# Routed experts on one core: the second product's tiles alternate with the next expert's first product, and small experts use one PSUM bank per unit

## The chip, the cores and the metric

The kernel runs on one core of a Trainium2 chip. The metric is the device time of one execution in microseconds, as the median of several executions. A profiled execution gives the trace that is read below; its times are microseconds from the start of its span.

## The reference, cut to what matters

The kernel computes one layer of a hybrid encoder for 1024 tokens of width 1024: a mixing half (recurrent heads and stick-breaking attention), which the change does not touch, and then 32 routed experts, of which each token uses four. For the experts the reference reads:

```python
def expert_block(args):
    tok, gate, e = args
    xb = xt[tok]
    hid = xb @ w1[e] + b1[e]                                  # 1024 -> 2048
    glu = jnp.minimum(hid[:, :D_FF_EXPERT], SWIGLU_LIMIT)
    lin = jnp.clip(hid[:, D_FF_EXPERT:], -SWIGLU_LIMIT, SWIGLU_LIMIT)
    act = glu * jax.nn.sigmoid(SWIGLU_ALPHA * glu) * (lin + 1.0)
    return (act @ w2[e] + b2[e]) * gate[:, None]              # 1024 -> 1024
out = jax.ops.segment_sum(y.reshape(n_rows, d), row_tok, num_segments=n_tok)
```

All weights are float32, 12.6 MB for one expert, and every expert's weights are read once. The precision is kept by splitting: a weight is a high part (`whi`, 32-bit) plus a low part (`wlo`, bf16), and the rows of an expert likewise.

## The kernel before, in words

Experts are sorted by their number of tokens, and each rank has a fixed capacity `c` of slots: 128 for the 13 smallest, 136 to 184 for the other 19. The kernel takes them in the order `ORDER`, largest and smallest in turn, so that for the first 26 experts one with more than 128 slots alternates with one of 128; the last six all have more than 128. Within this order `j` counts the experts.

An expert's weights come as six tiles of 2 MB: four of the first product, `(j, 1, q)` with q = 0 to 3 (q = 0 and 2 are the gate side, 1 and 3 the linear side of the two halves of the hidden width), and two of the second product, `(j, 2, 0)` and `(j, 2, 1)`. Each tile is two units, h = 0 and 1, and the list of units is the program order. The text writes A0 to A3 for the first product's tiles of an expert, S0 and S1 for the second's. The list `order` in `expert_units` (L1362 to L1367) is before: A1 A2 A3 of expert j, A0 of expert j + 1, then S0 S1 of expert j.

What happens for a unit, and where:

- `w_load` (L1371) issues a tile's load on SyncE's queue. There are WRAW = 4 raw buffers, so the load of a tile waits until the tile four places before it in the list is free. A first-product tile is free when VectorE has made the low parts of both its units (`next_lo`, L1538); a second-product tile is free only when TensorE has finished its second unit (`experts`, L1585 to L1588), since its raw form is itself multiplied. Loads are issued in the list's order.
- `w_hi` (L1411, ScalarE) makes the high part three units ahead of its use, `w_lo` (L1429, VectorE) the low part two units ahead. The first unit of S0 needs neither; it multiplies the raw weights.
- `first` (L1431) multiplies a first-product unit: for each of two blocks b of 128 hidden columns eight matmuls with the high weights over 2c columns (L1439) and eight with the low weights over c columns (L1443). Its accumulator `hid` is two PSUM banks, one for each block, and there are two such buffers, so that a unit waits until the unit two before it has been read out. The readout is two ScalarE activations (L1449) and one VectorE addition (L1450).
- `gated` (L1452) makes the activations after q = 1 and q = 3; `second` (L1480) multiplies by the second weights (L1500), and for an expert of more than 128 slots the remaining slots by the raw weights (L1506), and then scales and scatters the rows to the output (L1513 to L1522, GpSimd's indirect DMA with addition).
- `rows` (L1279) finds, beside A0 of expert j, which tokens expert j + 1 gets: a count by matmuls (L1308), some small VectorE steps, and an indirect DMA that gathers the rows (`xg`, L1327, GpSimd). `x_transpose` (L1331) turns those rows by TensorE transposes (L1344), the first group right behind the second unit of A1 in the program.

All of this is written in one program order; a planner then lays out each engine's instruction list, with its own estimates of durations, and every engine runs its list strictly in that order. PSUM is full: `hid` 4 banks, `ey` 2, `er` 1, `xt` 1, and the last is shared by the counts and the transposes.

Of the kernel before, what the change touches and what calls it, by code (L numbers as in the profile page):

```python
# [9 lines left out]
FT = mybir.dt.float32  # L10
# [17 lines left out]
NE = 32  # L28
# [86 lines left out]
class Trunk:  # L115
# [1241 lines left out]
    def expert_units(self, xs):  # L1357

        order = [(0, 1, 0)]  # L1362
        for j in range(NE):
            order += [(j, 1, q) for q in (1, 2, 3)]
            if j + 1 < NE:
                order.append((j + 1, 1, 0))
            order += [(j, 2, 0), (j, 2, 1)]  # L1367
        tiles = [Box(x=xs[j], w=w, q=q, i=i, raw=None) for i, (j, w, q) in enumerate(order)]
        return tiles, [Box(t=t, h=h) for t in tiles for h in range(2)]

# [60 lines left out]
    def first(self, u, pool, psum):  # L1431

        nc, x, t = self.nc, u.t.x, u.t
        half, g = divmod(t.q, 2)
        c, f = x.c, 8 * g + 4 * half + 2 * u.h
        ps = psum.tile([128, 2, 512], FT, name="hid", bufs=2)
        for b in range(2):
            for k in range(ND):
                nc.tensor.matmul(ps[:, b, :2 * c], u.hi[:, k, b * 128:(b + 1) * 128],  # L1439
                                 x.X2[:, k].rearrange("p a c -> p (a c)"), start=k == 0, stop=False)  # L1440
        for b in range(2):
            for k in range(ND):
                nc.tensor.matmul(ps[:, b, :c], u.lo[:, k, b * 128:(b + 1) * 128], x.xb[:, k, :],  # L1443
                                 start=False, stop=k == ND - 1)
        if u.h == 0:
            x.t[g] = pool.tile([128, 4, c], FT, name="ht", bufs=3, tag="ht")
        dst = x.t[g][:, 2 * u.h:2 * u.h + 2]
        for b in range(2):
            nc.scalar.activation(dst[:, b], ps[:, b, c:2 * c], AF.Identity, bias=x.bias[:, f + b:f + b + 1])  # L1449
        nc.vector.tensor_tensor(dst, dst, ps[:, :, :c], op=OP.add)  # L1450
# [29 lines left out]
    def second(self, u, pool, psum):  # L1480


        nc, x, t = self.nc, u.t.x, u.t
        first, last = t.q == u.h == 0, t.q == u.h == 1
        n1 = self.rest(x.c)
        nj = 128 // n1 if n1 else 0
# [365 lines left out]
```

## Time and profile before

| | |
|---|---|
| time, median of 3 executions | 2505.66 us (2494.64 to 2509.85) |
| time of the profiled execution | 2492.26 us |
| its span | 2490.4 us |
| TensorE matmul busy | 2346.1 us, 94% of the span |
| VectorE busy | 1977.9 us, 79% |
| ScalarE busy | 1573.8 us, 63% |
| mean granted TensorE clock | 0.969 |
| the units of the experts | from about 1088 us to about 2482 us |

The median tells the time; the profiled execution tells where it goes. Its own time is 13.4 us below the median, so a sum that is made on its rows is carried over to the median as a difference.

### The profile page before, as it was taken

The page shows a single profiled execution, that of the slowest core. Times are in us where ns is not written, and L with a number is a line of the kernel's source. Part 1 is how long each engine was busy: PE and PEld are TensorE (multiplying, and loading weights), DVE is VectorE, ACT ScalarE, POOL GpSimd, SP SyncE. Part 2 cuts the span into 40 slices and gives each one's busy share as a digit, 9 for nine tenths or more (in the row PEclk, how much of TensorE's full clock was granted, in tenths as well). Part 3 has the DMA queues.
Part 4 walks back from the last instruction along what each step waited for, and adds up shares of the span by engine and source line. Part 5 has one row for each costly group of instructions (what it writes and reads, how often), then busy time and mean ns, then how long its engine had stood idle before and what let it go on. Part 6 is the DMA issues. An engine that isn't in the chain of part 4 may idle for free. (4 is left out here: it accounts for less than half of the span.)

```text
span 2490.4 us, 49823 instructions
## 1 busy us (share of the span) xinstructions
PE 2346.1 (94%) x19973; PEld 1770.9 (71%) x19973; DVE 1977.9 (79%) x3639; ACT 1573.8 (63%) x2467; POOL 239.6 (10%) x182
## 2 busy tenths in 40 slices
PE   6889999999999899979999999999999999999997
PEld 2456676667676665667787787878788878887875
DVE  5567668669687767678888898898899989998885
ACT  3525556557676645346676676777677767776673
POOL 0000000000000000001111112111111112121111
PEclk8989999999999799979999999999999999999999
DMA  8774343333232312567798898889899989998994
GB/s 294 255 243 125 106 115 112 107 97 92 73 105 73 107 45 89 185 212 279 280 350 280 290 363 314 319 310 346 310 325 333 362 310 329 345 350 292 317 339 129
DMA packets 321007, 579.57 MB, mean 233 GB/s; under 512 B 46527, under 2 KB 110021, under 8 KB 320741
## 3 DMA queue, kind: packets, MB, share of 16 engines
q1 hardware_dynamic: 304768, 532.21, 60.1%
q0 software_dynamic: 14304, 43.53, 7.0%
q8 instruction: 159, 2.61, 0.4%
q10 hardware_dynamic: 1700, 0.61, 0.1%
q14 instruction: 76, 0.61, 0.1%
HBM read 517.69 MB, written 58.61 MB: 231 GB/s over the span
## 5 line engine op out<-in xcount | busy, mean ns | idle before, releaser
L1411 ACT ACTIVATE whi<-wraw 128x2048 fp32r<-128x2048 f32 (+1 forms) x361 | 675.4, 1876 | 376.1 <-PE ey L1500 158.3
L1429 DVE TENSOR_TENSOR wlo<-wraw,whi 128x2048 bf16<-128x2048 f32 (+1 forms) x361 | 805.4, 2234 | 112.0 <-PE ey L1500 67.9
L1439 PE MATMUL hid<-X,whi 128*128 128x256 f32 (+7 forms) x4096 | 628.9, 305 | 38.0 <-DVE ht L1450 36.0
L1439 PEld LDWEIGHTS hid<-X,whi 128*128 128x128 f32 x4096 | 561.4, 191 | 74.3 <-issue 63.9
L1443 PE MATMUL hid<-xb,wlo 128*128 128x128 bf16 (+7 forms) x4096 | 299.1, 226 | 0.0
L1443 PEld LDWEIGHTS <-wlo 128*128 128x128 bf16 x4096 | 251.9, 98 | 18.2
L338 PE MATMUL zps<-hhi,zwlo 128*128 128x512 f32 x416 | 246.5, 592 | 0.0
L336 PE MATMUL zps<-hhi,zwhi 128*128 128x512 f32 x416 | 188.5, 453 | 20.8 <-DVE zlast L380 8.0
L1449 ACT ACTIVATE ht<-hid,b1r 128x128 f32<-128x128 f32 (+7 forms) x496 | 158.6, 373 | 17.0 <-PE hid L1443 17.0
L337 PE MATMUL zps<-hlo,zwhb 128*128 128x512 bf16 x416 | 167.9, 404 | 1.4 <-DVE hlo L247 1.4
L1500 PE MATMUL ey<-whi,ah 128*128 128x512 f32 x384 | 143.9, 456 | 0.0
L1327 POOL DMA_INDIRECT xg<-h2d,si x49 | 79.1, 1614 | 573.8 <-PE ey L1500 321.6
L1500 PE MATMUL ey<-wraw,act 128*128 128x512 f32 x256 | 125.6, 611 | 1.3 <-SPq L1826 1.3
L1515 POOL DMA_INDIRECT out_dram<-ey,si x32 | 104.4, 3262 | 206.2 <-DVE ey L1513 177.4
L1450 DVE TENSOR_TENSOR ht<-ht,hid 128x256 f32<-128x256 f32 (+7 forms) x256 | 114.3, 447 | 10.4 <-ACT ht L1449 8.9
L1500 PE MATMUL ey<-whi,al 128*128 128x512 f32 x384 | 120.6, 395 | 0.0
L336 PEld LDWEIGHTS zps<-hhi,zwhi 128*128 128x128 f32 x416 | 82.4, 198 | 53.2 <-issue 21.4
L337 PEld LDWEIGHTS <-zwhb 128*128 128x128 bf16 x416 | 42.1, 101 | 93.2 <-issue 87.9
L1500 PE MATMUL ey<-wlo,ab 128*128 128x512 bf16 x384 | 99.6, 382 | 0.0
L1500 PEld LDWEIGHTS ey<-whi,ah 128*128 128x128 f32 x384 | 70.9, 189 | 39.4 <-issue 23.8
L514 DVE TENSOR_TENSOR_SCAN se<-se 128x128 f32<-128x128 f32 (+3 forms) x96 | 92.9, 971 | 0.7
L244 ACT ACTIVATE zwhi<-zwraw 128x1024 fp32r<-128x1024 f32 x50 | 52.8, 1055 | 61.1 <-PE zps L336 46.4
(475 smaller groups left out, 4124.8 us busy)
## 6 DMA issues: line engine op xcount, KB each, us to landing
wraw<-in_exp_w_dram SPq DMA_DIRECT2D x189, 2048.0 KB, 12.1
zwraw<-in_w_in_dram SPq DMA_DIRECT2D x50, 512.0 KB, 4.1
aw<-in_ada_w_dram SPq DMA_DIRECT2D x32, 512.0 KB, 5.3
zr<-zo SPq DMA_DIRECT2D x28, 256.0 KB, 3.6
zs<-zo SPq DMA_DIRECT2D x24, 256.0 KB, 2.1
nx<-in_x_dram SPq DMA_DIRECT2D x8, 512.0 KB, 7.3
awh<-in_ada_w_dram SPq DMA_DIRECT2D x8, 512.0 KB, 4.9
mx<-in_x_dram SPq DMA_DIRECT2D x16, 256.0 KB, 3.1
```

Of the source, the lines that this page charges most:

```text
L336: nc.tensor.matmul(ps, hi[:, k], self.hhi[:, k, s], start=k == 0, stop=False)
L337: nc.tensor.matmul(ps, hb[:, k], self.hlo[:, k, s], start=False, stop=False)
L338: nc.tensor.matmul(ps, lo[:, k], self.hhi[:, k, s], start=False, stop=k == ND - 1)
L514: nc.vector.tensor_tensor_scan(er, er, er, initial=carry, op0=OP.add, op1=OP.bypass)
L1411: nc.scalar.activation(dst[:, k], src[:, k], AF.Copy)
L1429: nc.vector.tensor_tensor(dst[:, k], src[:, k], hi[:, k], op=OP.subtract)
L1439: nc.tensor.matmul(ps[:, b, :2 * c], u.hi[:, k, b * 128:(b + 1) * 128], x.X2[:, k].rearrange("p a c -> p (a c)"), start=k == 0, stop=False)
L1443: nc.tensor.matmul(ps[:, b, :c], u.lo[:, k, b * 128:(b + 1) * 128], x.xb[:, k, :], start=False, stop=k == ND - 1)
L1449: nc.scalar.activation(dst[:, b], ps[:, b, c:2 * c], AF.Identity, bias=x.bias[:, f + b:f + b + 1])
L1450: nc.vector.tensor_tensor(dst, dst, ps[:, :, :c], op=OP.add)
L1500: nc.tensor.matmul(x.ps[n], a[:, j, :128], w[:, j, n * 512:(n + 1) * 512], start=first and m == 0, stop=last and m == len(products) - 1)
L1515: nc.gpsimd.indirect_dma_start(out=rows, out_offset=bass.IndirectOffsetOnAxis(ap=x.idx[:, 0:1], axis=0), in_=y, in_offset=None, compute_op ...
```

## The change

The list of tiles becomes: the four first-product tiles of expert 0, and then for every expert j: A0 of expert j + 1, S0 of expert j, A1 of expert j + 1, S1 of expert j, A2 and A3 of expert j + 1. So the two second-product tiles of an expert no longer follow each other. For experts of at most 128 slots the accumulator is allocated once for a tile (two units) and each unit uses one of its two banks, half a bank for each block of 128 columns; the eight high and eight low matmuls of the first block are then finished before those of the second block begin. Larger experts keep their accumulator and their order of matmuls. The numbers of buffers, the loads, the readouts and everything else stay as they are.

```diff
-        order = [(0, 1, 0)]
+        order = [(0, 1, q) for q in range(4)]
         for j in range(NE):
-            order += [(j, 1, q) for q in (1, 2, 3)]
-            if j + 1 < NE:
-                order.append((j + 1, 1, 0))
-            order += [(j, 2, 0), (j, 2, 1)]
+            n = [(j + 1, 1, q) for q in range(4)] if j + 1 < NE else []
+            order += [*n[:1], (j, 2, 0), *n[1:2], (j, 2, 1), *n[2:]]
...
-        ps = psum.tile([128, 2, 512], FT, name="hid", bufs=2)
-        for b in range(2):
+
+        small = c <= 128
+        if u.h == 0 or not small:
+            t.ps = psum.tile([128, 2, 512], FT, name="hid", bufs=2)
+        ps = t.ps[:, u.h].rearrange("p (b n) -> p b n", b=2) if small else t.ps
+
+        def high(b):
             for k in range(ND):
                 nc.tensor.matmul(ps[:, b, :2 * c], u.hi[:, k, b * 128:(b + 1) * 128],
                                  x.X2[:, k].rearrange("p a c -> p (a c)"), start=k == 0, stop=False)
-        for b in range(2):
+
+        def low(b):
             for k in range(ND):
                 nc.tensor.matmul(ps[:, b, :c], u.lo[:, k, b * 128:(b + 1) * 128], x.xb[:, k, :],
                                  start=False, stop=k == ND - 1)
+
+        for part, b in ((high, 0), (low, 0), (high, 1), (low, 1)) if small else ((high, 0), (high, 1), (low, 0), (low, 1)):
+            part(b)
```

## Rows read from the trace of the kernel before

**Rows 1.** Engines' busy time over 1150 to 2450 us, sum of four stretches:

```profile
sum 1300.00, PE 1262.12 PEld 1039.02 DVE 1146.99 ACT 920.87 POOL 221.18; mean PE 315.53 PEld 259.75 DVE 286.75 ACT 230.22 POOL 55.30
```

**Rows 2.** TensorE's groups, 1150 to 2450 us; busy, mean ns, idle before, releaser:

```profile
L1439 PE MATMUL hid<-X,whi 128*128 128x256 f32 x1632 | 234.7, 295 | 29.1 <-DVE ht L1450 28.8
...
L1439 PE MATMUL hid<-X,whi 128*128 128x288 f32 x512 | 79.4, 306 | 1.6 <-DVE ht L1450 1.5
L1439 PE MATMUL hid<-X,whi 128*128 128x272 f32 x464 | 67.0, 295 | 5.8 <-DVE ht L1450 5.7
```

**Rows 3.** TensorE's list in time around one stall; start, duration, idle before it:

```profile
1691.31 1.20 PE L1439 MATMUL hid<-X,whi 128*128 128x256 f32 x8
1692.35 1.07 PE L1443 MATMUL hid<-xb,wlo 128*128 128x128 bf16 x16
1696.25 2.26 PE L1439 MATMUL hid<-X,whi 128*128 128x256 f32 x9 [2.83 <-DVE ht L1450]
```

**Rows 4.** ScalarE's list in time around the same stall:

```profile
1692.92 1.91 ACT L1411 ACTIVATE whi<-wraw 128x2048 fp32r<-128x2048 f32 x1 [3.57 <-DMA wraw<-in_exp_w_dram]
...
1695.04 0.61 ACT L1449 ACTIVATE ht<-hid,b1r 128x128 f32<-128x128 f32 x2
```

**Rows 5.** SyncE's issues of weight loads, in time:

```profile
1673.21 0.37 SPq L1382 DMA_DIRECT2D wraw<-in_exp_w_dram  x1
1680.73 0.37 SPq L1382 DMA_DIRECT2D wraw<-in_exp_w_dram  x1
```

**Rows 6.** TensorE's list in time, end of S0 and of S1, and two units:

```profile
1661.28 0.63 PE L1308 MATMUL xt<-aux,oh 128*128 128x5 bf16 x16
...
1671.09 1.94 PE L1506 MATMUL er<-wraw,act 128*32 128x256 f32 x32
...
1680.49 2.17 PE L1439 MATMUL hid<-X,whi 128*128 128x256 f32 x16
...
1683.38 2.15 PE L1439 MATMUL hid<-X,whi 128*128 128x256 f32 x16
1685.38 1.07 PE L1443 MATMUL hid<-xb,wlo 128*128 128x128 bf16 x16
1686.28 0.61 PE L1344 MATMUL xt<-ident,xg 128*128 128x128 f32 x4
```

**Rows 7.** Stretches: length, engines busy (instructions), granted clock, DMA share, GB/s:

```profile
1650.00:1666.00 16.00, 16.00 (x166) 14.95 (x166) 15.32 (x26) 13.82 (x22) 0.00 (x0) 1.00 1.01 387
1666.00:1674.00 8.00, 8.00 (x55) 4.38 (x54) 7.52 (x17) 3.24 (x4) 2.96 (x2) 1.00 0.20 56
```

**Rows 8.** One stretch of 50 us with a lower granted clock, same columns:

```profile
1650.00:1700.00 50.00, 47.03 (x430) 38.92 (x430) 42.88 (x64) 33.70 (x49) 8.31 (x4) 0.97 0.86 308
```

**Rows 9.** TensorE's list in time from a count of rows to its transposes:

```profile
1625.23 0.34 PE L1308 MATMUL xt<-aux,oh 128*128 128x5 bf16 x8
...
1630.66 0.82 PE L1500 MATMUL ey<-whi,ah 128*128 128x512 f32 x2
...
1636.15 2.70 PE L1439 MATMUL hid<-X,whi 128*128 128x320 f32 x16
...
1643.32 0.60 PE L1344 MATMUL xt<-ident,xg 128*128 128x128 f32 x4
```

**Rows 10.** GpSimd's list in time: gathers (L1327) and the scatter behind one:

```profile
1630.08 1.00 POOL L1327 DMA_INDIRECT xg<-h2d,si  x1 [21.77 <-issue]
1638.01 3.37 POOL L1515 DMA_INDIRECT out_dram<-ey,si  x1 [6.93 <-DMA xg<-h2d,si]
1670.74 1.00 POOL L1327 DMA_INDIRECT xg<-h2d,si  x1 [29.35 <-PE ey L1500]
```

**Rows 11.** A readout that waited for its matmuls: TensorE, ScalarE and VectorE in time:

```profile
1703.45 1.07 PE L1443 MATMUL hid<-xb,wlo 128*128 128x128 bf16 x16
...
1704.55 0.63 ACT L1449 ACTIVATE ht<-hid,b1r 128x128 f32<-128x128 f32 x2 [1.84 <-PE hid L1443]
...
1707.10 0.41 DVE L1450 TENSOR_TENSOR ht<-ht,hid 128x256 f32<-128x256 f32 x1
```

## The prediction

> **What bounds the kernel now.** I read the stretches first, since the change touches only the experts. Over 1300 us of them TensorE is busy for 1262.12, VectorE for 1146.99 (88%) and ScalarE for 920.87 [rows 1]: the stage goes at TensorE's pace, and what can be won without taking work away is its 37.88 us of idle time. The groups of TensorE by shape say where that idle time lies: 28.8 us before the high matmuls of experts with 128 slots, 5.7 and 1.5 before those with 136 and 144, none worth naming elsewhere, and all of it ended by the readout's addition on VectorE, that is, by a full accumulator [rows 2]. TensorE's list in time has the 28.8 us as 13 stalls of 1.5 to 2.8 us, one in each small expert, of which one stands in [rows 3].
>
> What stands behind that releaser is read from the lists in time around one of them. TensorE ends a unit, then stands for 2.83 us [rows 3]. ScalarE had meanwhile waited 3.57 us for a weight tile, and the readout that TensorE needed was queued behind that wait on ScalarE; it began at 1695.04 [rows 4]. The tile's load had been issued at 1680.73 [rows 5], a quarter of a microsecond after TensorE finished S1 [rows 6]: it needed S1's raw buffer. The load before it was issued at 1673.21, right after the end of S0 at 1673.03 [rows 5, 6]. So both second-product tiles hold their buffers until TensorE has gone through them, one behind the other, and the loads starve: the DMA engines move 387 GB/s up to 1666 us and 56 in the eight microseconds after it [rows 7], and then the tiles come late. It is a bunching of loads, not a lack of bandwidth.
>
> **The change part by part.**
>
> *The order.* By the buffers' rule the load of tile i waits for tile i - 4. Before, A3 and then the next A0 wait for S0 and S1, which end 7.5 us apart (1673.03 and 1680.49 [rows 6]), and A0 is wanted two tiles after S1's end. After, S0 lets in A3, and the next A0 follows it at once; S1 lets in the next S0, which lies four tiles ahead. From the end of S0 to A3's first unit lie A1, S1 and A2, six units. At 2.9 us for a small unit (1680.49 to 1683.38 [rows 6]) that is over 17 us, minus 1.9 for the high part [rows 4], while the late load took 12.2 (1680.73 to 1692.92 [rows 4, 5]). ScalarE wants the high part some three units earlier, about 9 us after the issue, but it only holds back readouts that TensorE needs two units later. So no load should come later than the readouts can bear, and I take the small experts' 28.8 us as gone. What replaces them as the last is TensorE's own work: VectorE at 88% and ScalarE at 71% [rows 1] have room. The 7.2 us of the last large experts [rows 2] stand in a run with no small expert in it; their bounds are 0 and 7.2, and I take half, 3.6.
>
> *The clock.* After the stall of 2.83 us nine matmuls took 2.26 us where eight took 1.20 before it [rows 3]: 0.9 us lost in them, the engine at 1.2 instead of 2.4 GHz for a while. Four stretches of 50 us, each with one of the longer stalls, show 0.97 [rows 8], which is 1.5 us at most. Between 0.9 and 1.5 I take 1.3, four times: 5.2 us, gone with the stalls.
>
> *The bank per unit.* It gives a small expert's unit three or more units of distance to the readout in its way instead of two. That is a second cover for the same 28.8 us and is not counted twice. Its cost: TensorE changes from high to low and back once more in each unit. Eight high matmuls behind such a change take 1.04 us (1691.31 to 1692.35 [rows 3]), sixteen take 2.00 (1683.38 to 1685.38 [rows 6]), so the last eight take 0.96 and the change costs 0.08. There are 13 experts with 8 units, 104 changes: 8.3 us, on the engine that sets the pace, with nothing to hide it. The low part is wanted one microsecond earlier in the unit; VectorE makes it two units ahead, which covers that.
>
> *What else is moved.* The transposes of expert j + 1 stand behind A1, and between the count of rows and A1 there is now S0 alone, no longer S0 and S1. For a small next expert the transposes began 18.1 us after the count (1625.23 to 1643.32), of which S1 takes 5.5 (1630.66 to 1636.15 [rows 9]): 12.6 remain. The rows had landed by 1638.01, when the scatter queued behind them on GpSimd went on [rows 10]: 12.8 after the count. For a large next expert it is 25.0 (1661.28 to 1686.28) minus 7.5 for S1 [rows 6], 17.5 us, and the gather is issued 9.5 us after the count and lands up to 7.9 later (as 1630.08 to 1638.01 [rows 10]): 17.4. So the distance shrinks to about zero. If the count also moves behind A0's second unit, which it now precedes, 2.9 us more go, so the wait lies between 0 and 2.8 us for each of 30 gathers. Behind a waiting transpose stands all of TensorE's list. I take 0, since the gather will be issued just before S0 lets the loads in, on DMA engines that are then little used; the upper end is 84 us. The scatters on GpSimd and the loads on SyncE keep their order.
>
> **Sum.** -28.8 - 3.6 - 5.2 + 8.3 = -29.3 us. The profiled execution's 2492.26 us would become 2463; from the median of 2505.66 it is 2476 us, 1.2% less. The three times of before lie 15 us apart, so within 1% (25 us) counts as no change.
>
> **The rivals.**
>
> *The transposes wait for their rows.* Slower. Place: TensorE in front of the first transposes (L1344), ended by the gather's DMA. At the full 2.8 us it gives 2476 + 84 = 2560; it decides from 1.0 us for each gather, where the 29.3 are used up, and ends above 1% from 1.8 us. For it: the two margins of about zero. Against it: the planner may lay later matmuls in front of the transposes, and the gather is issued before the loads. 0.20, of which 0.05 stays within 1%.
>
> *The two halves of the accumulator count as one buffer*, so that the change doesn't do what it says. A readout of block 0 lies in another bank than block 1, and yet it started at 1704.55 when all sixteen low matmuls of the unit, begun at 1703.45, were through [rows 11]. If matmuls into the second bank likewise wait for the first bank's readout, each of 52 second units waits at least 0.63 + 0.41 us [rows 11]; in A0 and A1 the planner has units of S to put between, so 26 of them count: 27 us, 2503. With nothing between it is 54 and 2530. 0.12, of which 0.02 is above 1%.
>
> The Trainium skill speaks against this rival (PSUM — Partial Sum Buffer, PSUM bank collisions raise a hardware error): it asks for a guard by bank and quadrant, and has an engine reading one bank while TensorE writes another run clean. By that rule nothing on the chip asks for the wait and 2476 stands; the row above shows a wait for the whole of the two-bank tile, and no row shows the reverse, a write beside a readout of the same tile.
>
> *The stalls come back from VectorE.* At 88% and in strict order it may miss a readout by itself once the loads are in time. Half of the stalls stay: 2476 + 16 = 2492. 0.13.
>
> *More is won.* All 7.2 us of the large experts go, and the alternation spreads VectorE's low parts, four tiles of A in a row becoming three, so that the other small waits go too and half of the changes from high to low are hidden in them: 2460 to 2470. 0.10.
>
> **How the numbers follow.** The forecast has 0.45, of which 0.05 stays within 1%, since it lies only 4 us beyond. Faster by over 1%: 0.40 + 0.10 = 0.50. Slower: 0.15 + 0.02 = 0.17. The rest is 0.33. The range reaches down to 2455, the best case with all bounds and some 5 us of spread, and up to 2535, which takes in the second rival whole and the first up to 2 us for each gather; what it leaves out is the heavy end of the first and the scatter of the median, together 0.2.
>
> **What would show it.** Right: the idle time before L1439 by VectorE's readout is near zero, ScalarE's waits for `wraw` are short, issues of loads come in pairs with no stretch at 56 GB/s before a late tile, and the group of 128x256 matmuls costs some 8 us more between its starts. Wrong: idle time before L1344 with a gather as its releaser, or before the second unit of a small tile with its own first readout as releaser.

## The result, and the profile after

The changed kernel takes 2514.6 us (median of 12 runs) where the kernel before takes 2499.1 (12 runs on the same chip): a ratio of 1.0066, with an interval of 1.0048 to 1.0083. That is 0.7% slower, under the 1% that counted as a change, but outside the uncertainty, and on the other side of the forecast of 2476. One of the 12 runs took 5650 us and is left out of the ratio; nothing here explains it. The profiled execution has a span of 2512.50 us against 2490.43; the profile of before is a quick one among its runs (2492.26 us, 6.8 under the median).

TensorE's groups by shape, 1150 to 2450 us, after (they answer to [rows 2]):

```profile
L1442 PE MATMUL hid<-X,whi 128*128 128x256 f32 x1605 | 246.4, 296 | 6.5 <-DVE ht L1457 6.2
L1447 PE MATMUL hid<-xb,wlo 128*128 128x128 bf16 x1608 | 125.3, 221 | 7.8 <-DVE wlo L1427 7.8
...
L1442 PE MATMUL hid<-X,whi 128*128 128x320 f32 x512 | 85.8, 321 | 5.5 <-DVE ht L1457 5.1
L1442 PE MATMUL hid<-X,whi 128*128 128x288 f32 x512 | 80.8, 312 | 10.3 <-DVE ht L1457 10.3
L1442 PE MATMUL hid<-X,whi 128*128 128x304 f32 x384 | 63.5, 320 | 6.3 <-DVE ht L1457 6.2
...
L1344 PE MATMUL xt<-ident,xg 128*128 128x128 f32 x278 | 43.5, 275 | 5.2 <-DMA xg<-h2d,si 5.1
```

and the sum of four stretches over the same time (as [rows 1]):

```profile
sum 1300.00, PE 1248.22 PEld 1025.95 DVE 1127.82 ACT 907.80 POOL 186.17; mean PE 312.05 PEld 256.49 DVE 281.96 ACT 226.95 POOL 46.54
```

The small experts' idle time before the high matmuls fell from 28.8 us to 6.2, nearly as forecast, and what is left is of another kind (below). But the large experts, which had 7.2 us before ([rows 2]: 5.7 and 1.5), now have 24.5 (5.1, 10.3, 6.2 of it in the three rows), the small ones wait 7.8 us for low parts, which they never did, and 5.1 us are waits for gathered rows. TensorE is busy for 1248.22 us of the 1300, less than the 1262.12 of [rows 1].

**The second half waits for the first.** This is TensorE's list in time for a small expert's tiles A2 and A3, after:

```profile
1601.09 1.22 PE L1442 MATMUL hid<-X,whi 128*128 128x256 f32 x8
...
1604.44 1.19 PE L1442 MATMUL hid<-X,whi 128*128 128x256 f32 x8
1606.21 0.62 PE L1447 MATMUL hid<-xb,wlo 128*128 128x128 bf16 x8 [0.58 <-DVE wlo L1427]
...
1609.07 1.22 PE L1442 MATMUL hid<-X,whi 128*128 128x256 f32 x8 [0.78 <-DVE ht L1457]
...
1612.74 1.51 PE L1442 MATMUL hid<-X,whi 128*128 128x256 f32 x8
...
1615.99 2.60 PE L1442 MATMUL hid<-X,whi 128*128 128x320 f32 x16
...
1622.56 2.74 PE L1442 MATMUL hid<-X,whi 128*128 128x320 f32 x9 [2.84 <-DVE ht L1457]
```

and VectorE's, in the same time, a low part and the addition queued behind it:

```profile
1606.40 2.28 DVE L1427 TENSOR_TENSOR wlo<-wraw,whi 128x2048 bf16<-128x2048 f32 x1
1608.61 0.41 DVE L1457 TENSOR_TENSOR ht<-ht,hid 128x256 f32<-128x256 f32 x1
```

By the program's own numbers of tiles and weights, 1601.09 is A2's first unit, 1604.44 is A3's first, 1609.07 is A2's second, and 1612.74 A3's second. The addition that reads A2's first unit ends at 1608.61 + 0.41 = 1609.02, and A2's second unit starts 0.05 us later, though it writes the other bank. The list of instructions has the wait written out: the second unit's first matmul waits for VectorE (here A2 and A3 of another small expert).

```
12425 L1442 MATMUL hid_22457<-X2_21852,whi_22385 128x256 [waits DVE_49]
12463 L1442 MATMUL hid_22553<-X2_21852,whi_22453 128x256 [waits DVE_49]
```

Laid against the trace, instruction by instruction, all 52 second units of small experts' tiles begin after the first unit's addition, none less than 53 ns after it and 31 of them within 53 to 56 ns (the 35 in the expectation of E5 below is a miscount). In the list all 52 wait for VectorE. The planner knows this wait and puts A3's first unit between A2's units, which is the swapped order seen above; that unit is then wanted before its low part is there (the 0.58).

**The loads still come late.** SyncE's issues of weight loads, after:

```profile
1601.22 0.37 SPq L1386 DMA_DIRECT2D wraw<-in_exp_w_dram  x1
1601.85 0.37 SPq L1380 DMA_DIRECT2D wraw<-in_exp_w_dram  x1
```

ScalarE's list, after:

```profile
1614.37 0.39 ACT L1353 ACTIVATE xb<-xt 128x256 bf16<-128x256 f32 x1
1618.92 1.91 ACT L1409 ACTIVATE whi<-wraw 128x2048 fp32r<-128x2048 f32 x1 [4.16 <-DMA wraw<-in_exp_w_dram]
...
1621.35 0.60 ACT L1456 ACTIVATE ht<-hid,b1r 128x128 f32<-128x128 f32 x2
```

S1 of the expert before lets in the next S0 at 1601.22 (L1386 loads a second-product tile, L1380 one of the first product), and 0.63 us later follows A1 of the large expert. By the program's list the tile that ScalarE waits for here is this A1: it wants it from 1614.76 (1618.92 - 4.16), 12.9 us after its issue, and has it after 17.1. S0, issued first, was used at 1611.79 without a wait for its load. The loads are moved one behind the other: in the trace's DMA packets S0's (4 KB each) start up to 1609 and A1's (2 KB) only from 1608, and up to 1612 a scatter's packets go beside them. Behind ScalarE's wait is queued a readout (1621.35), and TensorE, now in the large expert's A0, stands for 2.84 us (1622.56). It is the stall of [rows 3, 4] in another place. Before, the late tile was the first of its pair: A0, issued at 1680.73 [rows 5], with S0's load right behind it:

```profile
1681.37 4.99 SPq L1388 DMA_DIRECT2D wraw<-in_exp_w_dram  x2
```

Over the whole stage ScalarE waits 74.6 us for weights, 46.2 of it for A1; before it was 65.2, 36.6 of it for A0. The median load takes 14.0 us to land instead of 12.1 (of the 50 whose landing the trace tells).

What a stall of that length does to the clock, in stretches of 10 us, after (length, engines busy, granted clock, DMA share, GB/s):

```profile
1610.00:1620.00 10.00, 9.71 (x95) 8.76 (x93) 8.55 (x9) 4.69 (x9) 2.24 (x1) 1.00 1.04 362
1620.00:1630.00 10.00, 7.44 (x43) 6.79 (x44) 5.47 (x8) 7.43 (x14) 0.00 (x0) 0.66 0.82 302
```

A mean of 0.66 is some 6.8 of the 10 us at 1.2 GHz, the rest at 2.4.

**The ledger.** For each profiled execution, from TensorE's list in time: the stage from the first matmul of the first product to the end of the last `ey` matmul; idle time (pauses over 0.1 us) by what ended it, readouts apart for small and large experts; work, which is the stage less the idle time; and the time in the stage at 1.2 GHz. In us; small items are left out of the middle columns.

| kernel | stage | idle | readouts small / large | low part | rows | X2 | work | at 1.2 GHz |
|---|---|---|---|---|---|---|---|---|
| before | 1386.1 | 39.7 | 28.8 / 7.2 | 0 | 0 | 1.3 | 1346.4 | 17.4 |
| after | 1414.2 | 52.5 | 6.3 / 24.5 | 7.8 | 5.2 | 6.9 | 1361.7 | 41.5 |
| e1 order alone | 1380.4 | 39.3 | 2.8 / 24.4 | 0 | 10.0 | 0.6 | 1341.1 | 14.1 |
| e2 bank alone | 1449.8 | 75.2 | 61.4 / 9.5 | 0 | 0 | 1.7 | 1374.6 | 85.7 |
| e3 more alternation | 1402.7 | 36.6 | 25.6 / 5.8 | 0 | 0 | 2.4 | 1366.1 | 31.1 |
| e4 spaced | 1468.9 | 83.5 | 0.3 / 2.9 | 0 | 37.0 | 11.2 | 1385.4 | 83.0 |
| e5 own banks, new order | 1393.2 | 41.6 | 0 / 2.5 | 0 | 35.2 | 2.8 | 1351.6 | 30.8 |
| e6 own banks, old order | 1378.5 | 31.9 | 0 / 9.8 | 0 | 0 | 21.3 | 1346.5 | 10.6 |
| e7 order, late transposes | 1371.2 | 29.9 | 7.9 / 4.6 | 0 | 0 | 16.5 | 1341.3 | 13.9 |
| e8 order, half loads | 1338.5 | 5.0 | 0.6 / 0.6 | 0 | 1.9 | 0.6 | 1333.5 | 3.8 |
| e9 own banks, late transposes | 1361.8 | 14.6 | 0 / 3.3 | 0 | 0 | 10.8 | 1347.3 | 10.4 |
| e10 own banks, early rows | 1361.0 | 17.2 | 2.5 / 7.9 | 0 | 4.8 | 1.3 | 1343.8 | 13.8 |
| e11 order, early rows | 1370.8 | 30.1 | 0 / 25.9 | 1.4 | 0 | 2.0 | 1340.7 | 24.1 |
| e12 after, half loads | 1347.6 | 7.3 | 0.3 / 0.6 | 0 | 0.6 | 0.6 | 1340.4 | 3.8 |

Against the order alone the changed kernel has 13.2 us more idle time and 20.6 more work. Of the time at 1.2 GHz TensorE is busy for 39.2 and 14.0 us; at half the clock it does half, so that an estimated 12.6 us of the work is the lower clock. 8.0 are left for the alternation of high and low matmuls. The same sum gives 2.7 for E2 and 3.0 for E6 against before, 3.1 for E5 against E1, 7.1 for E9 against E7 and 7.5 for E10 against E11.

### The profile page after: what moved, and what is told of

Same layout as the page of the kernel before. It is cut to its first block, busy times and chain, and to the rows that moved or that the text cites. A ratio compares the mean times of both kernels' runs of the same rounds, so it can differ in the third digit from the quotient of the medians.

```text
span 2512.5 us, 49732 instructions
## 1 busy us (share of the span) xinstructions
PE 2353.7 (94%) x19973; PEld 1776.9 (71%) x19973; DVE 1978.2 (79%) x3639; ACT 1577.4 (63%) x2467; POOL 206.8 (8%) x182
## 5 line engine op out<-in xcount | busy, mean ns | idle before, releaser
L1442 PE MATMUL hid<-X,whi 128*128 128x256 f32 (+7 forms) x4096 | 654.6, 309 | 39.1 <-DVE ht L1457 30.4
L1442 PEld LDWEIGHTS hid<-X,whi 128*128 128x128 f32 x4096 | 573.0, 193 | 85.9 <-issue 52.2
L1447 PE MATMUL hid<-xb,wlo 128*128 128x128 bf16 (+7 forms) x4096 | 320.7, 228 | 7.8 <-DVE wlo L1427 7.8
L1522 POOL DMA_INDIRECT out_dram<-ey,si x32 | 84.8, 2650 | 467.0 <-DVE ey L1520 465.7
L1327 POOL DMA_INDIRECT xg<-h2d,si x49 | 72.9, 1487 | 394.7 <-issue 156.2
L526 PEld LDWEIGHTS sbo<-sbv,sat 128*128 128x128 f32 x576 | 76.5, 195 | 18.4 <-ACT sat L524 9.5
```

The lines of the kernel that those rows point to most:

```text
L1522: nc.gpsimd.indirect_dma_start(out=rows, out_offset=bass.IndirectOffsetOnAxis(ap=x.idx[:, 0:1], axis=0), in_=y, in_offset=None, compute_op ...
```

## The experiments

All ratios are to the kernel before, timed on the same chip in the same session; the interval stands behind.

**E1 and E2, the two parts alone.** E1 is the kernel before with the first piece of the diff above alone (the order). E2 has the second piece alone (the accumulators and their order of matmuls); its list of tiles is that of before:

```diff
 E2, against the changed kernel
...
-            order += [*n[:1], (j, 2, 0), *n[1:2], (j, 2, 1), *n[2:]]
+            order += [(j, 1, q) for q in (1, 2, 3)]
...
+            order += [(j, 2, 0), (j, 2, 1)]
```

> The new order alone, accumulators as before. Theory P (parts: the loss is some 8 us of switches between high and low, some 9 us of lowered clock and some 12 us of new idle time, because loads issued in pairs share the DMA engines and a second-product tile still comes late): without the switches 8 us of the loss go, but the small experts lose the spare bank as well, so 0.2% to 0.6% slower than before, idle time before the high matmuls at 30 us or more. Rival B (the order does what was forecast and the bank with its split blocks does the harm): 1.0% to 1.4% faster than before, idle time under 10 us.

> The bank per unit alone, in the order of before. Theory P: the small experts' units get room, so most of the 28.8 us before their high matmuls go and 5 us of clock with them, against 8.3 us of switches: 0.7% to 1.0% faster than before. Rival B: VectorE misses the low parts that are now wanted earlier, and the stall only moves: within 0.3% of before or slower.

E1: 2488.5 us, 0.9951 (0.9932 to 0.9969). E2: 2555.2 us, 1.021 (1.019 to 1.023). The order is a gain and the bank a loss, in either order. Neither expectation was met: E1 lies between its two, with 27.2 us of waits for readouts where one had 30 or more and the other under 10, and E2 is slower, as its rival allowed, but without the waits for low parts that the rival gave as the reason. In E2, TensorE's list, ScalarE's and VectorE's around one of 13 stalls of 4.2 to 5.4 us:

```profile
1815.83 1.91 ACT L1411 ACTIVATE whi<-wraw 128x2048 fp32r<-128x2048 f32 x1 [4.02 <-DMA wraw<-in_exp_w_dram]
1817.64 1.13 ACT L1458 ACTIVATE ht<-hid,b1r 128x128 f32<-128x128 f32 x4
...
1818.28 0.94 DVE L1459 TENSOR_TENSOR ht<-ht,hid 128x256 f32<-128x256 f32 x2 [3.38 <-ACT ht L1458]
...
1818.85 2.90 PE L1444 MATMUL hid<-X,whi 128*128 128x256 f32 x12 [5.38 <-DVE ht L1459]
```

The late load is the one of before (4.02 us of waiting here, 3.57 in [rows 4]), and from its end to TensorE's start it takes the same 3 us (1815.83 to 1818.85; 1692.92 to 1696.25 in [rows 3, 4]). What differs is when TensorE ran dry: there 0.50 us after the wait's end (1692.35 + 1.07), here 2.36 before it (1818.85 - 5.38 = 1813.47). That is 2.9 us, one small unit, earlier. Two units' readouts are queued behind the wait (the four activations), and neither A2's second half nor A3 may start without them: A2's second half waits for its first, A3 for the tile of A1, which comes free only with both of A1's units. The twelve matmuls after the stall are four of A3's first unit and eight of A2's second, as the planner had interleaved them. So the shared tile lets TensorE run one unit less ahead, and each late load costs 4.2 to 5.4 us instead of 1.5 to 2.8. The stage then spends 85.7 us at 1.2 GHz.

**E3, more alternation in the kernel before.** Two banks for each unit as before, but every unit in the order high, low, high, low:

```diff
-        for b in range(2):
...
-        for b in range(2):
...
+        for part, b in ((high, 0), (low, 0), (high, 1), (low, 1)):
+            part(b)
```

> The kernel before, with the two blocks of every first-product unit of all experts finished one after the other (high, low, high, low) in their two banks: 256 more changes from high to low and back. At 0.08 us each on the engine that sets the pace: 20 us or 0.8% slower. If the change is hidden behind weight loads or idle time: within 0.2%. If a low part that is wanted earlier makes TensorE wait for VectorE: over 1% slower, with idle time in front of the low matmuls.

1.0011 (0.9994 to 1.0029), that is 2.7 us (-1.5 to 7.2) for 256 units, where 0.08 each would have made 20. The alternation doesn't explain the loss of 15.5: the changed kernel has it in 104 units, which by this is at most 2.9 us.

**E4, the second product spread further.**

```diff
 against the kernel before
-        order = [(0, 1, 0)]
+        order = [(0, 1, 0), (0, 1, 1)]
...
-            order += [(j, 1, q) for q in (1, 2, 3)]
+            order += [(j, 1, 2), (j, 2, 0), (j, 1, 3)]
...
-            order += [(j, 2, 0), (j, 2, 1)]
+            order.append((j, 2, 1))
+            if j + 1 < NE:
+                order.append((j + 1, 1, 1))
```

> Another order, accumulators as before: a second-product tile after every second first-product tile (A2, S0 of the same expert, A3, A0 of the next, S1, A1 of the next), so that the two held buffers lie three tiles apart throughout. Theory P (bunched frees of the raw buffers make the loads come in pairs and late): issues of loads are never over 12 us apart, ScalarE's waits for weights go, 20 to 35 us less than before, 0.8% to 1.4% faster. Rival (the distance from the gather to its transposes sets the wait, or VectorE does): no faster than before, with idle time before the transposes or the low matmuls.

1.0295 (1.0273 to 1.0317): the rival, by more than it said. Of the stalls behind readouts 3.2 us are left, but it isn't shown that spacing the second product's tiles mends the loads. They are still issued up to 15.0 us apart (1619.70 and 1634.69), and ScalarE still waits 75.6 us for weights (65.2 before). TensorE stands elsewhere meanwhile, mostly before the transposes: 37.0 us for gathers, 19.3 for a cause that the profile doesn't name and 11.2 for X2, of 83.5 us in all; and 83.0 us at 1.2 GHz go with it.

**E5 and E6, a bank of its own for each unit.** The accumulators are four tiles of one bank; a small unit takes one, a large unit two (the matmuls and readouts are adapted to that):

```diff
-        if u.h == 0 or not small:
-            t.ps = psum.tile([128, 2, 512], FT, name="hid", bufs=2)
...
+        if small:
+            one = psum.tile([128, 512], FT, name="hid", bufs=4)
+            ps = [one[:, :256], one[:, 256:]]
+        else:
+            ps = [psum.tile([128, 512], FT, name="hid", bufs=4) for _ in range(2)]
...
```

> The changed order with four accumulators of one bank each: a small expert's unit has one for itself, a large expert's unit takes two (its readout's addition on VectorE is then two instructions). In the trace of the changed kernel all 52 second units of a small expert's tiles begin after the addition that reads out the first unit, 35 of them within 53 to 56 ns of it. Theory 'the halves are served one after the other': the shared tile is the harm, so with own tiles the waits of the second units go, the planner lays the units in their natural order again, and the time falls to that of the order alone or a little under: ratio 0.988 to 0.997 to the kernel before. Rival 'the alternation of high and low matmuls and the low parts wanted earlier are the harm': both are still here, so the time stays near the changed kernel's, ratio 1.003 to 1.010, with TensorE still waiting some 8 us for low parts.

> The order of before with the same four accumulators of one bank. The stalls of before lie in small experts (28.8 us), behind readouts that are held up on ScalarE. Theory 'the halves are served one after the other': with a tile of its own each unit has three units of distance instead of two, so a good part of the 28.8 us goes: 5 to 12 us of stalls in small experts stay and the ratio is 0.985 to 0.994. The shared tile in the same order had 1.021. Rival 'the alternation of matmuls is the harm': 1.010 to 1.025 again.

E5: 2496.9 us, 0.998 (0.996 to 1.000). E6: 2486.5 us, 0.9937 (0.9912 to 0.9962). In the old order the same alternation of matmuls, but with own tiles, is 0.6% faster than before where the shared tile was 2.1% slower: the shared tile is the harm, and the rival falls. No stall of a small expert is left in E6 (the expectation had 5 to 12 us); 21.3 us of waits for X2 are new. The planner lays the units in their natural order again, and in E5's list of instructions 39 of 52 second units wait for ScalarE's high part alone:

```
12571 L1444 MATMUL hid_22726<-X2_22060,whi_22603 128x256 [waits Activation_49]
```

Twelve wait for an instruction of VectorE, and one for nothing. In E5's trace all 52 begin before the first unit's readout has ended.

In the new order E5 fell a little short of its bracket (0.988 to 0.997). Its groups of TensorE show where the time went:

```profile
L1444 PE MATMUL hid<-X,whi 128*128 128x256 f32 x1600 | 242.5, 293 | 0.0
...
L1344 PE MATMUL xt<-ident,xg 128*128 128x128 f32 x282 | 46.4, 284 | 38.2 <-DMA xg<-h2d,si 35.2 <-DVE X L1354 2.6
```

No wait of a small unit is left, and TensorE runs into the gathered rows instead, 35.2 us in 18 waits.

**E7, E9, E10 and E11, the rows.** E7 and E9 begin the next expert's transposes one first-product unit later, on E1 and on E5; E10 and E11 count and gather the rows one tile earlier, on E5 and on E1:

```diff
 E7, E9
-                if (t.q, u.h) == ((1, 0) if x.j else (2, 1)) and x.j + 1 < NE:
+                if (t.q, u.h) == ((1, 1) if x.j else (2, 1)) and x.j + 1 < NE:
 E10, E11
-                if t.q == 0 and 1 <= x.j < NE - 1:
-                    self.rows(xs[x.j + 1], pool, psum, u.h)
+                if t.q == 0 and x.j == 1:
+                    self.rows(xs[2], pool, psum, u.h)
+                if t.q == 3 and 1 <= x.j < NE - 2:
+                    self.rows(xs[x.j + 2], pool, psum, u.h)
```

> The changed order with the accumulators of before, and the first transposes of the next expert one unit later, behind the second unit of A1's tile instead of its first. In the run with the order alone 8 of 30 experts waited for gathered rows, 10.0 us in all, the longest 2.6; one unit later is 2.9 us. Theory 'the gather has lost its cover': the 10 us go, nothing else moves, ratio 0.989 to 0.993 against 0.995 with the order alone. Rival 'what waits here comes back a step later' (the transposed rows are now ready too late for the next expert's first unit): ratio 0.994 to 1.000, with TensorE waiting for the subtraction that makes X2.

> The changed order, own accumulators of one bank and the first transposes one unit later. With the own banks in the new order 18 of 30 experts waited for gathered rows, 35.2 us in all, none for readouts to speak of (2.5); one unit later is 2.9 us for each. Theory 'own banks do cover the late loads, and the time that they win stood in the waits for rows': about 20 to 25 of the 35 us go, ratio 0.986 to 0.992 to before. Rival 'the loads set the pace, and every wait that is taken away comes back at the next instruction': the idle time stays at 35 us or more in another place, ratio 0.995 to 1.000.

> As before this one, but the transposes in their old place and the count and the gather of an expert's rows one tile earlier: with the last tile of the expert two before, ahead of a second product, instead of with the first tile of the expert one before. Theory 'the gather has lost its cover': with some 12 us more the waits for rows fall under 5 us, nothing takes their place, ratio 0.982 to 0.990. Rival 'the loads set the pace': ratio 0.993 to 1.000, the 35 us of idle time then stand before the high or low matmuls, by ScalarE or VectorE.

> The changed order with the accumulators of before and the count and the gather one tile earlier. With the order alone 10.0 us were waits for rows and 27 for readouts. Theory 'the gather has lost its cover': the 10 us go and the 27 stay, ratio 0.989 to 0.993. Rival 'the loads set the pace': the readouts' waits grow by what the rows' waits lose, ratio 0.994 to 0.998.

| kernel | us | ratio |
|---|---|---|
| E7 order, late transposes | 2476.5 | 0.9903 (0.9868 to 0.9938) |
| E9 own banks, late transposes | 2461.9 | 0.9863 (0.9833 to 0.9894) |
| E10 own banks, early rows | 2465.3 | 0.9873 (0.9844 to 0.9901) |
| E11 order, early rows | 2472.4 | 0.9895 (0.9866 to 0.9924) |

The edit of E7 and E9 does more than their expectations say. The first transposes move from behind A1's second unit to behind A2's first, and S1 stands between these, so that they begin not 2.9 but some 8 to 10 us later: 22.0 to 24.7 us after the count for small next experts in E7, where E1 has 13.1 to 15.0.

All four times lie in the brackets of the theory that the gather had lost its cover. E11 does just what it gave: no wait for rows, 25.9 us for readouts as in E1 (27.2). E7 is less pure than expected: the rows' 10.0 us go, the readouts' waits fall from 27.2 to 12.5 (nothing in the expectation gave that), and 14.9 us of waits for X2 come, as the rival had it. In E10 the waits for rows fall from 35.2 us to 4.8, but those for readouts rise from 2.5 to 10.4, where the theory had nothing. In E9 all 35.2 go, and 10.8 for X2 are there. E9 is faster than both kernels, by 1.4% than before; its groups of TensorE, the first row and those with the most idle time:

```profile
L1444 PE MATMUL hid<-X,whi 128*128 128x256 f32 x1609 | 247.7, 294 | 0.0
...
L1444 PE MATMUL hid<-X,whi 128*128 128x304 f32 x384 | 61.0, 310 | 2.0 <-DVE ht L1463 1.8
...
L1344 PE MATMUL xt<-ident,xg 128*128 128x128 f32 x282 | 45.2, 278 | 7.5 <-DVE X L1354 7.2
```

**E8 and E12, half loads.** On E1 and on the changed kernel:

```diff
-        raw = pool.tile([128, ND * 512], FT, name="wraw%d" % (t.i % WRAW), bufs=1)
+        short = t.i >= 2 * WRAW
+        raw = self.tiles[t.i - WRAW].whole if short else pool.tile([128, ND * 512], FT, name="wraw%d" % (t.i % WRAW), bufs=1)
...
-            nc.sync.dma_start(t.raw, w[:, t.q * 4:(t.q + 1) * 4, :])
+            n = 2 if short else 4
+            nc.sync.dma_start(t.raw[:, :n], w[:, t.q * 4:t.q * 4 + n, :])
```

> The changed order with the accumulators of before; from the ninth weight tile on only half of each tile is loaded (the other half keeps an older expert's weights, so the output is another). All other instructions are the same. Theory 'the stalls that are left come from loads that land late': the some 25 us that TensorE waits for readouts in the run with the order alone go down to under 8 and the ratio is 0.980 to 0.987. Rival 'they come from VectorE's own load': they stay at 20 us or more, ratio 0.993 to 0.997.

> The changed kernel (both parts of the change); from the ninth weight tile on only half of each tile is loaded (the other half keeps an older expert's weights, so the output is another). It is to be compared with the same for the order alone, 2441.8 us (0.976). Theory 'the halves are served one after the other, and that costs where a readout is late': with loads in time the readouts are in time, the waits of second units shrink to a few us and the planner's order does no harm: ratio 0.976 to 0.981. Rival 'the halves cost by themselves, whatever the loads do' (0.5 to 0.8 us for each of some 26 second units, and the matmuls that alternate): 0.984 to 0.990.

E8: 2441.8 us, 0.9757 (0.9713 to 0.9801). The waits for readouts are gone (27.2 us to 1.3), and so are ScalarE's waits for weights (109.0 us in E1, none in E8): these stalls are the loads'. The gain is larger than the bracket. The DMA engines' share falls from 0.91 to 0.55. The stretch from 1150 to 2450 us of E8, with its DMA share and GB/s at the end:

```profile
1150.00:2450.00 1300.00, 1268.33 (x10842) 1046.79 (x10902) 1149.12 (x1651) 929.66 (x1286) 218.36 (x153) 1.00 0.55 176
```

and of E1:

```profile
1150.00:2450.00 1300.00, 1258.37 (x10723) 1041.23 (x10782) 1141.69 (x1636) 925.37 (x1276) 200.28 (x151) 1.00 0.91 323
```

The waits for rows go nearly too (10.0 to 1.9), but not because the gathers land sooner. From issue to landing they take 7.1 us in the median of E1 (first line) and 7.4 in E8:

```profile
DMA to landing us min/median/max: 4.2/7.1/9.7
DMA to landing us min/median/max: 4.3/7.4/9.4
```

They are issued sooner. In E1, one of the experts that waited, from the count to the transposes:

```profile
1618.91 0.34 PE L1308 MATMUL xt<-aux,oh 128*128 128x5 bf16 x8
...
1621.33 2.28 DVE L1427 TENSOR_TENSOR wlo<-wraw,whi 128x2048 bf16<-128x2048 f32 x1
...
1624.64 0.14 DVE L1318 CAST si<-sa 128x1 int32<-128x1 f32 x1
1625.57 1.00 POOL L1327 DMA_INDIRECT xg<-h2d,si  x1 [12.71 <-PE ey L1498]
1633.18 0.66 PE L1344 MATMUL xt<-ident,xg 128*128 128x128 f32 x4 [0.66 <-DMA xg<-h2d,si]
```

The same expert in E8:

```profile
1604.00 0.34 PE L1308 MATMUL xt<-aux,oh 128*128 128x5 bf16 x8
...
1608.80 1.00 POOL L1327 DMA_INDIRECT xg<-h2d,si  x1 [10.87 <-PE ey L1502]
...
1617.45 0.60 PE L1344 MATMUL xt<-ident,xg 128*128 128x128 f32 x4
```

The gather is issued 6.7 us after the count in E1 and 4.8 in E8. A low part of 2.28 us stands in E1 among VectorE's steps that make the row numbers; it does so for all 8 experts that waited in E1 and all 18 in E5. For half loads the planner laid its lists anew (VectorE's differs from E1's in 54 places), and this low part is gone from there. So E8 is no test of the loads alone where the rows are concerned.

E12: 2451.6 us, 0.9827 (0.9789 to 0.9866), between the two brackets, so its time alone doesn't decide. Its list does: the idle time is 7.3 us and no second unit waits for a readout to speak of, so with loads in time the shared tile costs no waits. What it still costs in the traces is work, 1340.4 against E8's 1333.5 at the same clock, 6.9 us. (The medians lie 9.8 us apart, the ratios, from two sessions, 17.)

## Why the prediction was wrong, point by point

The forecast was -29.3 us and 15.5 more were measured, 45 us apart. By E1 (and the ratios) about 25 of these are the order's (forecast -37.6 with the large experts and the clock, measured -12) and about 20 the bank's (forecast +8.3, which leaves +28).

**The order** was right in its sign and in its place, and wrong in its size. The small experts' 28.8 us went to 2.8 in E1. The sentence that failed is "no load should come later than the readouts can bear". It was worked out for the loads that S0 and S1 let in, A3, the next A0 and the next S0. A1's load, which stands right behind S0's in the list of tiles, was left out, and that is the one that comes late: 17.1 us from issue to use in the row above, wanted after 12.9. In E1 51.2 of ScalarE's 109.0 us of waits for weights are for A1 and 36.6 for S0. The 12.2 us were no price for it either: they were taken from the first load of a pair, and before, too, a load with others in front of it (S1) took 15 to 18 us where ScalarE waited for it. So 24.4 us of stalls came up in the large experts, where I had looked only for what was there before. E8 shows that they are the loads': with half the bytes they go.

**The bank per unit** is the step that turned the sign. I took it for a second cover, "three or more units of distance", at a price of 8.3 us. The price was of the right order at best: 6.9 us by E12 against E8, 8.0 by the ledger's sum for the changed kernel against E1, but some 3 in three other pairs, and at most 2.9 by the time of E3. The cover was not there. The rival "the two halves of the accumulator count as one buffer" came true, to which I gave 0.12: all 52 second units wait for the first unit's readout. My 27 us for it is about the 26 us between E1's and the changed kernel's medians (2488.5 and 2514.6, sessions apart; 29 by the ratios), but that is luck: it came by another way. I had priced a wait of 0.63 + 0.41 us at 26 units; those waits came to 6.3 us, eight of 0.78 and a ninth of 0.1, since the planner fills them with the next tile's first unit. Against E1 the traces have, besides, 7.8 us of waits for low parts that this filling wants early ("VectorE makes it two units ahead, which covers that" failed too), some 6 more for X2 whose cause stays open, 5 less for rows, and the estimated 12.6 of the lower clock and 8.0 of alternation. That a tile is held until both its units are read out shows in E2, where it makes the stalls longer. E5 and E6 show that the shared tile is the cause: with own tiles in the same four banks, and the same alternation, no wait of a small unit for a readout or a low part is left.

The Trainium skill (PSUM — Partial Sum Buffer, PSUM bank collisions raise a hardware error), which I held against this rival, asks for a guard by bank and quadrant only. E5 agrees with it as far as the chip goes: with two tiles all 52 second units began before the first unit's readout had ended. The wait is the program's, laid by the tile, and the rule says nothing about that.

**The clock.** I counted 5.2 us as won. In E1 the time at 1.2 GHz fell from 17.4 to 14.1, worth 1.7; in the changed kernel it rose to 41.5. Some 7 us of that are probably not the change's: a first stretch at 1.2 GHz reaches 10.8 us into the stage there and 3.9 in E1, but 10.4 in E11, which has E1's order and accumulators.

**The moved gather.** I took 0 between 0 and 84 us. E1 has 10.0 us in 8 of 30 experts, the changed kernel 5.2, and E5, which runs ahead faster, 35.2. The margins "of about zero" were worked out rightly; the error was to take the lower end, with a gather issued 4.9 us after a small next expert's count as in [rows 9, 10]. Where E1 waits for such an expert it is issued 6.1 to 7.0 us after it, in E5 7.2 to 8.7, behind a low part on VectorE; to land it takes its 7 to 8 us as before. That ate about half of what the order won: E11, without these waits, is at 0.9895 where E1 is at 0.9951.

**The large experts' 3.6 us** didn't come; see the order.

**"More is won"** was nearly right about what could be had, not about this kernel: its 2460 to 2470 were 36 to 46 us less than before, and E9 is 33 us faster than before in its own session (2461.9 against 2494.6). "The stalls come back from VectorE" stays without support: E8 has VectorE at 1149.12 of 1300 us and hardly any stall.

What stays open is why the readouts' waits fell in E7, and what exactly an alternation costs. An accumulator with half of its tile released by itself was not tried, nor E9 and E10 together.

## What to carry to other kernels

Two halves of one tile are one buffer until the trace or the list of waits shows otherwise; if a unit is to have a bank for itself, give it a tile for itself. A load's time to land, taken from the first of a pair, is a lower end for the second; go through every load in the order of issue, also those that stand behind a held one, and look for the stall at the next readout in line, not only where it was. And a step that gains time draws down every margin of about zero: after each one, look what is now just too late (here the rows, worth 0.5% on E1 and 1.2% on E5 once they were moved).

## What the runs showed of the hardware that was not expected

A gather's time to land was no shorter with half the bytes of loads beside it: its median was 7.1 us in E1, with the DMA engines' share at 0.91, and 7.4 in E8 at 0.55. Two loads that were issued 0.63 us apart were moved one behind the other: S0's packets start from 1602 to 1609, A1's from 1608 to 1619, and A1 was there 17.1 us after its issue. And the lowered clock grew faster than the idle time: E2's 13 stalls of 4.2 to 5.4 us, 61.4 in all, went with 85.7 us of the stage at 1.2 GHz, while the 28.8 us of before, in 13 stalls of up to 2.8 and a short one, went with 17.4: twice the idle time, five times the lowered clock.
